# A one-core transformer block with a mixture of experts: the second half's routing and sort moved behind and between the experts' products, and the end without products that place x

## The chip, the cores and the metric

One NeuronCore of a Trainium2 chip runs the whole kernel. The metric is the time of one execution on the device in microseconds (us); the median of three runs is shown.

## What is computed

One block on 512 tokens of width 1024: a norm, an input projection, forgetting attention beside a gated recurrence, an output projection, and then a mixture of experts. The change touches the last part only:

```python
h2 = rmsnorm(x, ffn_norm[l]).reshape(b * s, d)
# hierarchical_moe: group_p = softmax(h2 @ w_group + b_group), the top 1 of 4 groups (weight g_w)
#   inner = h2 @ w_inner[group] + b_inner, softmax, the top 2 of 8 experts, renormed
for g in range(N_GROUPS):
    hg = silu(einsum('nd,edf->nef', t, w_gate[g])) * einsum('nd,edf->nef', t, w_up[g])
    y = y + einsum('nef,efd->nd', hg * combine[:, g, :, None], w_down[g])
x = x + y.reshape(b, s, d)
return rmsnorm(x, final_norm)
```

Each of the 32 experts has 3 MB of weights (gate, up, down: 1024 x 256 floats each), 100 MB in all, read once.

## The kernel before, in words

**Tokens and experts.** The tokens are four tiles t of 128, in two halves hf (t 0 and 1, t 2 and 3). For each half an expert has 32 places (CAP). The experts are worked off in eight quads (g, q) of four experts: g 0 is the first group; the other 24 experts are ranked by their load (`sort_parts`, L899), and the last group (LIGHT, the lightest) needs only one set of places for both halves. Should an expert get more tokens than places, a branch at the very end (L1297) works the rest off; the number `ovi` that decides it is made at L1285 to L1293.

**A quad.** `gather_parts` (L951) makes one-hot matrices s16 (f16) and s (fp32r) from the tokens' places and multiplies h2 with them, in four parts of two k-blocks each; h2 (scaled) is held as a high part h2h (fp32r, ACT) and a low part h2l (f16), so a part is eight products. The results go to the tile xg, evicted by DVE (parts 0 and 2) and ACT (1 and 3). `gate_up` multiplies xg with the gate and up weights, one k-block of 128 at a time (four experts a block; 8 blocks). `places` puts the one-hots and the weights c into the layout of the experts' rows (sT, cw), `hidden` is silu and product (ACT, DVE), `hidden_T` transposes it, `down` multiplies with w_down, `split_y` splits its result into two fp32r parts (ACT, DVE), `scatter` multiplies back to tokens and DVE adds to xs, which holds x.

**Routing.** `fill_router` (L624) makes a tile's router logits lg and h2; for t 3 the low part is an ACT copy h2s and a POOL subtraction (L656 to L659). `route(1)` (L679) ranks the second half's groups and experts (`ranks`, L670; go, o), makes the 0/1 mask msk, counts with products on PE (stri, onesb) the tokens before each token, which DVE turns into counts cnt and places pos1, and then computes the experts' weights c16. Its small tiles lie in the pool `work`.

**The order.** Where `pinned` is 1, PE's instructions stay in program order; with 2, those of DVE and ACT do as well. What comes between the router of t 3 and the loop over the quads is written in the string FIRST (L49, loop at L1135): "hk" is k-block k of half h of quad (0, 0), "gather" a part of half 1's gather, "rank" the counting products and the one-hots, "weights" the rest of route(1), the release of `work`, the pool `ring_b` in its place, and the loads of quad (0, 0)'s down weights, "sort" the next of the five parts of `sort_parts`. The loop over the quads (L1155) goes on with half 0's blocks 4 and up, places, hidden.

**Weights.** All weight loads stand on SP's queue in program order, as loads of 512 KB into slots of 1 MB: 12 in `slot`, 4 in `slot_m`, 2 in `slot_b`. slot_b lies in `ring_b`, over tiles of `work`. A load waits for its slot and for the one eight before it. The loads of a ranked expert need its number, which SP reads from `ids`, a result of the sort.

**The end** (L1240 to L1297). In the last quad four products `place_x` (one for each t, identity times x, the second 512 columns) put x into PSUM, between k-blocks 4 to 7; the last scatter adds to it there. `square_out` (L1076) sums squares on ACT, `rsqrt_parts` (L1094) makes the factors, `write_out` (L1082) scales and writes eight pieces of 256 KB. Four ACT copies then bring x back to xs for the branch, and the overflow number is made.

## Time and profile before

| | us |
|---|---|
| three runs: lowest, median, highest | 511.38, 511.52, 512.45 |
| the profiled execution | 510.38 |
| its span | 508.6 |
| PE (TensorE products) busy | 470.3 (92%) |
| DVE (VectorE) busy | 291.4 (57%) |
| ACT (ScalarE) busy | 193.5 (38%) |
| POOL (GpSimd) busy | 47.1 (9%) |

Clock granted to PE, mean over the span: 0.979. The DMA engines read 118.45 MB of HBM, at 237 GB/s over the span. Times in the rows below count from the span's start. An engine's idle time is put down to the one whose semaphore came last; idle time of an engine that others do not wait for costs nothing, and a share of busy time over the span says little about one stage, so stretches are read each by itself.

### The profile page before, as it was taken

Reading aid. Unit: us, or ns where it says so; the run is one execution under the profiler, and the core shown is the slowest. Engines: PE = TensorE matmul, PEld = TensorE weight load, DVE = VectorE, ACT = ScalarE, POOL = GpSimd, SP = SyncE. Lnnn points to the kernel's source line nnn. Section 1 sums busy time; section 2 is a strip of 40 time slices with the busy share of each in tenths; the row PEclk is TensorE's granted clock in tenths of the full one; section 3 lists DMA queues with packets and bytes.
Section 4 is the critical chain, followed back from the end, with each engine's and each line's share of the span. In section 5 each row is a group of like instructions: output and inputs, shape, how many; then the busy total and the mean of one; then the engine's idle time right before and its main releaser. Section 6 shows DMA issues by size and latency. Waiting matters only on the chain.

```text
span 508.6 us, 9411 instructions
## 1 busy us (share of the span) xinstructions
PE 470.3 (92%) x3525; PEld 287.0 (56%) x3525; DVE 291.4 (57%) x757; ACT 193.5 (38%) x406; POOL 47.1 (9%) x90
## 2 busy tenths in 40 slices
PE   7999999979999999999849999999999999998970
PEld 4997777758887877678414435434354333642330
DVE  4868654396996578967772525436263353353343
ACT  6454157736773357555402113111131111211045
POOL 4400000230121022300100000000000000000030
PEclk9999999999999999999879999999999999998996
DMA  8687332123244400327943999999999999999924
GB/s 315 108 205 197 81 86 78 47 75 93 83 145 187 167 0 1 100 69 275 381 170 117 386 378 378 417 409 410 404 386 409 406 413 371 388 411 382 333 104 168
DMA packets 58578, 121.20 MB, mean 238 GB/s; under 512 B 10753, under 2 KB 29217, under 8 KB 58530
## 3 DMA queue, kind: packets, MB, share of 16 engines
q1 hardware_dynamic: 58528, 120.56, 65.7%
q8 instruction: 29, 0.48, 0.4%
q14 instruction: 19, 0.16, 0.1%
q10 hardware_dynamic: 2, 0.00, 0.0%
HBM read 118.45 MB, written 2.10 MB: 237 GB/s over the span
## 4 chain that ended last, share of the span: by engine, by line
PE 81%; DVE 10%; ACT 6%; issue 1%; DMA 1%; POOL 0%; DVEq 0%; ACTq 0%; POOLq 0%
PE ps_mm L69 46%; PE ps_lg L69 17%; PE ps_tr L69 10%; PE ps_pv L69 4%; PE ps_tr L79 3%; DVE hold L393 1%; DVE hg L88 1%; ACT hold L94 1%; ACT slot L94 1%; DMA xs<-in_x_dram 1%; DVE srt L82 1%; ACT hg L94 1%; DVE s L82 1%; DVE slot L82 0%; DVE msk L88 0%
## 5 line engine op out<-in xcount | busy, mean ns | idle before, releaser
L69 PE MATMUL ps_mm<-slot 128*128 128x512 f32 (+1 forms) x576 | 120.3, 366 | 2.9 <-DVE kS L82 2.8
L69 PE MATMUL ps_mm<-slot,xg 128*32 128x512 f32 x688 | 106.6, 613 | 7.2 <-DVE xg L82 6.6
L69 PEld LDWEIGHTS ps_mm<-slot 128*128 128x128 f32 x576 | 96.2, 192 | 22.2 <-issue 5.1
L69 PEld LDWEIGHTS ps_mm<-slot,xg 128*32 128x32 f32 x688 | 26.6, 112 | 45.5 <-issue 35.6
L82 DVE TENSOR_TENSOR xs<-xs,ps_lg 128x512 f32<-128x512 f32 x56 | 34.8, 682 | 12.4 <-PE ps_lg L69 12.2
L82 DVE TENSOR_TENSOR slot<-slot 128x1024 fp32r<-128x1024 f32 (+1 forms) x27 | 32.9, 1221 | 13.4 <-ACT slot L94 13.4
L94 ACT ACTIVATE hg<-ps_mm 128x256 f32<-128x256 f32 x14 | 5.4, 383 | 89.1 <-PE ps_mm L69 83.8
L88 DVE SCALAR_TENSOR_TENSOR hg<-hg,ps_mm 128x256 f32<-128x256 f32 x14 | 5.9, 421 | 56.2 <-ACT hg L94 56.2
L94 ACT ACTIVATE y<-ps_tr 128x512 fp32r<-128x512 f32 x26 | 15.5, 597 | 49.8 <-PE ps_tr L69 38.2
L69 PE MATMUL ps_lg<-y,sT 128*128 128x512 f32 x118 | 33.4, 421 | 1.1 <-ACT y L94 0.9
L69 PE MATMUL ps_lg<-s,hold 128*128 128x256 f32 x128 | 33.3, 367 | 0.5 <-ACT s L94 0.4
L69 PE MATMUL ps_lg<-s,h2l 128*128 128x256 f16 x128 | 32.2, 285 | 0.9 <-DVE s L82 0.9
L94 ACT ACTIVATE slot<-slot 128x1024 fp32r<-128x1024 f32 (+1 forms) x28 | 29.3, 1055 | 6.8 <-DMA slot<-in_w_in_dram 5.0
L69 PEld LDWEIGHTS ps_lg<-y,sT 128*128 128x128 f32 x118 | 19.9, 188 | 20.6 <-issue 10.9
L82 DVE TENSOR_TENSOR y<-ps_tr,y 128x512 fp32r<-128x512 f32 x26 | 17.9, 687 | 21.9 <-ACT y L94 21.9
L558 POOL TENSOR_TENSOR ql<-qT,qh 64x128 fp32r<-64x128 f32 x32 | 19.9, 622 | 110.5 <-ACT qh L94 96.3
L69 PE MATMUL ps_mm<-slot_m,xg 128*32 128x512 f32 x128 | 28.9, 593 | 0.0
L1080 POOL TENSOR_TENSOR slot<-xs,gfin 128x512 f32<-128x512 f32 x4 | 5.0, 1282 | 241.2 <-ACT slot L94 241.2
L69 PEld LDWEIGHTS ps_lg<-s,hold 128*128 128x128 f32 x128 | 26.0, 203 | 2.3 <-ACT s L94 2.3
L69 PE MATMUL ps_mm<-slot,hold 128*128 128x512 f32 x96 | 26.2, 409 | 0.0
L69 PE MATMUL ps_mm<-slot,oT 128*128 128x512 f32 x96 | 24.6, 402 | 0.5 <-DVE oT L82 0.5
L94 ACT ACTIVATE xg<-ps_lg,g8s 128x256 f32<-128x256 f32 x28 | 11.7, 470 | 33.0 <-PE ps_lg L69 32.9
(269 smaller groups left out, 747.2 us busy)
## 6 DMA issues: line engine op xcount, KB each, us to landing
slot<-in_w_gate_dram SPq DMA_DIRECT2D x50, 512.0 KB, 10.1
slot<-in_w_up_dram SPq DMA_DIRECT2D x50, 512.0 KB, 10.2
slot_m<-in_w_down_dram SPq DMA_DIRECT2D x24, 512.0 KB, 10.1
slot<-in_w_down_dram SPq DMA_DIRECT2D x24, 512.0 KB, 10.7
slot<-in_w_in_dram SPq DMA_DIRECT2D x16, 512.0 KB, 3.9
slot<-in_w_out_dram SPq DMA_DIRECT2D x8, 512.0 KB, 3.9
slot_m<-in_w_gate_dram SPq DMA_DIRECT2D x8, 512.0 KB, 11.4
slot_m<-in_w_up_dram SPq DMA_DIRECT2D x8, 512.0 KB, 10.7
```

Source lines behind the costliest of these rows:

```text
L69: pin(nc.tensor.matmul(out=out_, lhsT=lhsT, rhs=rhs, start=start, stop=stop))
L79: pin(nc.tensor.transpose(out=out_, in_=in_, identity=ident[0:n, 0:n]))
L82: return pin(nc.vector.tensor_tensor(out=out_, in0=a, in1=b, op=op), 2)
L88: pin(nc.vector.scalar_tensor_tensor(out=out_, in0=a, scalar=s, in1=b, op0=op0, op1=op1), 2)
L94: pin(nc.scalar.activation(out=out_, in_=in_, func=func, **kw), 2)
L393: nc.vector.tensor_tensor_scan(out=ti_[:, c, :], data0=tr_[:, c, :], data1=xc[:, c, :], initial=0.0, op0=ALU.mult, op1=ALU.add)
L558: nc.gpsimd.tensor_tensor(out=ql[own, hh], in0=src, in1=qh[own, hh].bitcast(F32), op=ALU.subtract)
L1080: nc.gpsimd.tensor_tensor(out=yo[t][:, sl], in0=src, in1=gfin[:, sl], op=ALU.mult)
```

## The change

1. FIRST is rewritten: six k-blocks of half 0 ahead of "rank", which now also finishes the router of t 3 (r3), releases `work`, opens `ring_b` and starts quad (0, 0)'s down loads; "sort" is the first two parts at once, and "weights" is what remains of route(1), behind the gathers and 13.
2. The low part of h2 of t 3 is one DVE instruction behind the one-hots, as for the other t, instead of ACT's h2s and POOL's subtraction.
3. route(1)'s small tiles move from `work` to the pool `moe` (under tags that are free then), so `ring_b` no longer lies over them; mg and the group's Exp come right behind msk.
4. The last three parts of the sort (the places of groups 1 to 3, posp) become `sort_places(g + 1)`, called in the pass with q 1 ahead of each group; the sort's middle part (light, more, over) and the overflow number stand in pass 1.
5. A gather's products for the second t of a half take the high part first; half 1's first gather is evicted by ACT alone.
6. Quad (0, 0)'s gate and up weights come with two k-blocks to a load (32 loads of 256 KB) instead of four (16 of 512 KB).
7. At the end place_x and the four copies go; the last scatter is added to xs by DVE; the first half of the second down product stands right behind the first down; PSUM tags follow.

```diff
-FIRST = "00 01 02 03 rank 04 05 weights sort gather sort 06 10 11 gather sort 12 gather sort 07 13 gather sort"
+FIRST = "00 01 02 03 04 05 rank 06 07 gather gather 10 11 sort gather 12 13 weights gather"
...
         if t == 3:
-            v = kd(w4("h2s"))
-            act(v, x_kp, AF.Copy, scale=invs[:, 0:1])
-            nc.gpsimd.tensor_tensor(out=lo, in0=v, in1=hi.bitcast(F32), op=ALU.subtract)
-        else:
-            stt(lo, x_kp, invs[:, 0:1], hi.bitcast(F32), ALU.mult, ALU.subtract)
+            yield
+        stt(lo, x_kp, invs[:, 0:1], hi.bitcast(F32), ALU.mult, ALU.subtract)
...
+        def two_bytes(shape, dt, name):
+            if hf:
+                return moe[0].tile(shape, dt, name=name, tag="hgT", bufs=2)
+            return work.tile(shape, dt, name=name, tag="msk" if name == "msk" else "si", bufs=1)
+        small_ = moe[0].tile([P, 136], F32, name="rt", tag="hg", bufs=1) if hf else work.tile([P, 136], F32, name="rt", bufs=1)
...
+    def sort_places(g):
+        r0 = first_rank(g)
+        t_ = ring_b[0].tile([P, 5, EG, NS], F16, name="sp", tag="y0", bufs=2)
+        sh = [P, NT, EG, NS]
+        p1 = pos1.rearrange("p t g e -> p t (g e)")[:, :, EG:]
+        tt(t_[:, 0], bc(rank1[0], [P, EG, NS], 1), bc(iota1[:, r0:r0 + EG], [P, EG, NS], 2), ALU.is_equal)
+        tt(t_[:, 1:], bc(p1, sh, 2), bc(t_[:, 0], sh, 1), ALU.mult)
+        with nc.allow_low_precision(reason="one number of a sum isn't zero"):
+            pin(nc.vector.reduce_sum(out=posp[0][:, :, r0:r0 + EG], in_=t_[:, 1:], axis=AX.X), 2)
...
-                terms = [(h, t, i) for h in hfs for t in range(2) for i in range(2)]
+                terms = [(h, t, i) for h in hfs for t in range(2) for i in ((0, 1), (1, 0))[t]]
...
-            if kk % 2:
+            if kk % 2 or by_act:
...
-    gus[0] = load_gate_up(experts(0, 0), 4)
+    gus[0] = load_gate_up(experts(0, 0), 2)
...
         if o == "rank":
             next(r1)
             s01 = next(g01)
-        elif o == "weights":
-            run(r1)
+            run(r3)
             work.release()
             ring_b.append(pool("ring_b"))
             dns[0] = load_down(experts(0, 0))
             sx[0, 1] = s01, next(g01)
+        elif o == "weights":
+            run(r1)
+        elif o == "sort":
             srt = sort_parts()
-        elif o == "sort":
+            next(srt)
             next(srt)
...
+            if i == 1:
+                run(srt)
+                ovf = small.tile([P, 1], F32, name="ovf", bufs=1)
...
+            if q == 1:
+                sort_places(g + 1)
             gu_k(0, range(4, KT))
...
-        if k >= 4:
-            place_x(k - 4, "pv" if k == 7 else "lg")
...
+    py1 = psum("tr")
+    down_mm(py1, hgT, dns[i], 1, [0])
+    pa, pb = ([psum("lg"), psum(tag)] for tag in ("lg", "mm"))
...
+    down_mm(py1, hgT, dns[i], 1, [1])
+    y1 = split_y(py1)
...
+    for t in range(2):
+        scatter_add(pc[t], t, 1)
+        square_out(t, 1, xs[:, t, h1])
+    for t in range(2):
+        scatter_add(pd[t], 2 + t, 1)
...
-    for t in range(NT):
-        act(xs[:, t, h1], pz[t], AF.Copy)
```

How the order of the engines moves, at the two places that the prediction speaks of and at the end. PE from the router of t 3 on: `ps_tr<-wr,h2T` is the router's product, `ps_mm<-slot,xg` with four products to a k-block the gate/up products, stri and onesb the counting products, `ps_lg<-s,...` a gather with the low part (h2l) and the high one (hold). Before:

```order
L69 MATMUL ps_tr<-wr,h2T 128x36 x8
L69 MATMUL ps_mm<-slot,xg_2523 32x512 x16
L69 LDWEIGHTS stri
L69 MATMUL ps_tr<-msk,stri 128x32
...
L69 MATMUL ps_tr<-msk,onesb 128x24
L69 MATMUL ps_mm<-slot,xg_2523 32x512 x8
L69 LDWEIGHTS h2l
L69 MATMUL ps_lg<-s_2664,h2l 128x256
L69 MATMUL ps_lg<-s_2663,hold_2441 128x256
```

and with the change:

```order
L69 MATMUL ps_tr<-wr,h2T 128x36 x8
L69 MATMUL ps_mm<-slot,xg_2530 32x512 x24
L69 LDWEIGHTS stri
L69 MATMUL ps_tr<-msk,stri 128x32
...
L69 MATMUL ps_tr<-msk,onesb 128x24
L69 MATMUL ps_mm<-slot,xg_2530 32x512 x8
L69 LDWEIGHTS h2l
L69 MATMUL ps_lg<-s_2671,h2l 128x256
L69 MATMUL ps_lg<-s_2670,hold_2432 128x256 x2
```

Six k-blocks stand ahead of the counting products instead of four, two behind them as before, and the gather takes its two high parts in a row.

DVE behind the counting products (cnt and pos read them; s is the one-hot, srt, rank, idf, ids the sort, xg the first gather's eviction). Before, the last of the sort and what follows it:

```order
L82 TENSOR_TENSOR c_1058<-go,cp 128x192
L82 TENSOR_TENSOR s_2664<-iota_500,pos_1057 128x256 x2
L88 SCALAR_TENSOR_TENSOR srt_2720<-cnt_1061,iota_500 128x24
...
L85 TENSOR_SCALAR ids<-idf 1x24
L931 TENSOR_REDUCE over<-pos_1057 128x1
...
L939 TENSOR_REDUCE posp<-srt_2774 128x4x8
L939 TENSOR_REDUCE posp<-srt_2791 128x4x8
...
L939 TENSOR_REDUCE posp<-srt_2813 128x4x8
L85 TENSOR_SCALAR ovf<-ovf 128x1
L82 TENSOR_TENSOR xg_2719<-ps_lg,g8s 128x512 x2
```

and with the change:

```order
L88 SCALAR_TENSOR_TENSOR msk<-rt 128x32 x2
L709 TENSOR_REDUCE rt<-lg 128x2
L82 TENSOR_TENSOR rt<-lg,rt 128x8
L82 TENSOR_TENSOR cnt_1061<-ps_tr,cnt_1060 128x24
L88 SCALAR_TENSOR_TENSOR pos_1057<-ps_tr,msk 128x64
L82 TENSOR_TENSOR s_2671<-iota_500,pos_1057 128x256 x2
L88 SCALAR_TENSOR_TENSOR h2l<-xs,invs,hold_2432 128x1024
L88 SCALAR_TENSOR_TENSOR srt_2732<-cnt_1061,iota_500 128x24
...
L85 TENSOR_SCALAR ids<-idf 1x24
L85 TENSOR_SCALAR rt<-rt 128x16 x2
```

The one-hots s come ahead of the weights (c), the low part h2l behind them, the sort up to ids next, then the weights (the small rt); posp and xg are gone from this stretch.

PE at the end, from the last gate/up products on (hgT stands in the down products, y in the scatter). Before:

```order
L69 MATMUL ps_mm<-slot,xg_4536 32x512 x2
L69 MATMUL ps_pv<-xs,ident 128x512
L69 MATMUL ps_tr<-ident,hg 32x128 x8
L69 MATMUL ps_mm<-slot,hgT 32x512 x8
L69 MATMUL ps_mm<-y_5032,sT_4959 128x512
L69 MATMUL ps_mm<-y_5033,sT_4959 128x512
```

and with the change:

```order
L69 MATMUL ps_mm<-slot,xg_4546 32x512 x2
L69 MATMUL ps_tr<-ident,hg 32x128 x8
L69 MATMUL ps_mm<-slot,hgT 32x512 x8
L69 MATMUL ps_tr<-slot,hgT 32x512 x4
L69 MATMUL ps_lg<-y_5034,sT_4969 128x512
L69 MATMUL ps_lg<-y_5035,sT_4969 128x512
```

The last place_x (ps_pv from xs) is gone, and four of the second down's products stand ahead of the first scatter.

## Rows read from the trace of the kernel before

**Rows 1.** The page: the busy line of TensorE (busy us, share of the span, instructions), the GB/s of the 40 slices, and from its DMA issues the last down's sixteen loads (count, KB each, median us from issue to landing).
```profile
PE 470.3 (92%) x3525; PEld 287.0 (56%) x3525; DVE 291.4 (57%) x757; ACT 193.5 (38%) x406; POOL 47.1 (9%) x90
...
GB/s 315 108 205 197 81 86 78 47 75 93 83 145 187 167 0 1 100 69 275 381 170 117 386 378 378 417 409 410 404 386 409 406 413 371 388 411 382 333 104 168
...
slot<-in_w_down_dram SPq DMA_DIRECT2D x16, 256.0 KB, 5.6
```

**Rows 2.** Busy time by stretches of 4 us around the second half's routing: the stretch, its length, busy us and instructions (x) of PE, PEld, DVE, ACT and POOL, the granted clock of PE as a share, the DMA engines' busy share and GB/s.
```profile
248.00:252.00 4.00, 1.77 (x19) 1.29 (x19) 3.45 (x11) 0.28 (x2) 2.34 (x1) 0.92 1.02 413
252.00:256.00 4.00, 3.57 (x20) 1.35 (x12) 3.62 (x18) 0.75 (x2) 0.00 (x0) 0.65 0.64 236
...
260.00:264.00 4.00, 0.07 (x4) 0.07 (x8) 3.88 (x8) 0.00 (x0) 0.00 (x0) 0.70 0.32 119
264.00:268.00 4.00, 4.00 (x19) 0.93 (x20) 0.00 (x0) 0.00 (x0) 0.00 (x0) 0.50 0.00 0
```

**Rows 3.** PE's timeline there: start us, us, engine, line, operation, out<-in, tile, count, and in brackets the idle time before it and who ended it. `ps_mm<-slot,xg` are gate/up products, `ps_tr<-msk,stri` is the first of rank's, `ps_lg<-ident,s` begins places, `ps_pv<-ident,hg` is hidden_T.
```profile
244.63 3.64 PE L69 MATMUL ps_mm<-slot,xg 128*32 128x512 f32 x32
250.51 0.19 PE L69 MATMUL ps_tr<-msk,stri 128*128 128x32 bf16 x1 [2.23 <-DVE msk L88]
...
250.76 3.63 PE L69 MATMUL ps_mm<-slot,xg 128*32 128x512 f32 x16
...
263.93 3.64 PE L69 MATMUL ps_mm<-slot,xg 128*32 128x512 f32 x16 [6.59 <-DVE xg L82]
...
269.69 1.07 PE L69 MATMUL ps_mm<-slot,xg 128*32 128x512 f32 x8 [0.62 <-ACT xg L94]
...
274.67 0.29 PE L69 MATMUL ps_lg<-ident,s 128*32 128x128 f16 x8
...
277.43 0.61 PE L69 MATMUL ps_pv<-ident,hg 128*32 128x128 f32 x16
```

**Rows 4.** The chain of waits, in order of time, at one gather part that ran without a wait (start us, us, what).
```profile
270.75 1.07 PE ps_lg L69 x8
```

**Rows 5.** The timelines of DVE, ACT and POOL, columns as in rows 3: the first half's msk, the low part of another t, and what the second half's routing has on these engines.
```profile
208.38 0.58 DVE L88 SCALAR_TENSOR_TENSOR msk<-o,go 128x32 bf16<-128x32 f32 x2
...
235.34 2.31 DVE L88 SCALAR_TENSOR_TENSOR h2l<-xs,invs,hold 128x1024 f16<-128x1024 f32 x1 [2.41 <-ACT hold L94]
...
243.03 0.84 ACT L94 ACTIVATE xg<-ps_lg,g8s 128x256 f32<-128x256 f32 x2 [1.28 <-PE ps_lg L69]
...
248.06 2.34 POOL L659 TENSOR_TENSOR h2l<-h2s,hold 128x1024 f16<-128x1024 f32 x1 [36.72 <-ACT h2s L94]
...
248.19 2.37 DVE L88 SCALAR_TENSOR_TENSOR msk<-o,go 128x32 bf16<-128x32 f32 x2
...
254.21 0.76 DVE L82 TENSOR_TENSOR s<-iota,pos 128x256 f16<-128x256 f16 x2
...
258.80 0.17 DVE L85 TENSOR_SCALAR ids<-idf 1x24 int32<-1x24 f32 x1
...
259.96 1.81 DVE L939 TENSOR_REDUCE posp<-srt 128x32 f16<-128x768 f16 x2
...
263.20 0.68 DVE L82 TENSOR_TENSOR xg<-ps_lg,g8s 128x512 f32<-128x512 f32 x1
```

**Rows 6.** The timeline of SP's DMA queue (the time is that of the issues): half 0's last weights, the first and last of the loads into slot_b, the next one, and the last quad's down weights.
```profile
213.37 0.43 SPq L104 DMA_DIRECT2D slot<-in_w_up_dram  x1
...
253.96 0.33 SPq L104 DMA_DIRECT2D slot_b<-in_w_gate_dram  x1
...
255.28 0.77 SPq L104 DMA_DIRECT2D slot_b<-in_w_up_dram  x1
273.69 0.33 SPq L104 DMA_DIRECT2D slot<-in_w_gate_dram  x1
...
466.98 14.38 SPq L104 DMA_DIRECT2D slot<-in_w_down_dram  x16
```

**Rows 7.** Busy time by stretches of 100 us, columns as in rows 2: most of the quads.
```profile
284.00:384.00 100.00, 98.77 (x964) 44.52 (x952) 46.11 (x104) 20.80 (x47) 0.00 (x0) 1.00 1.02 399
384.00:484.00 100.00, 95.64 (x897) 38.27 (x896) 39.98 (x97) 15.59 (x36) 0.00 (x0) 0.98 1.01 389
```

**Rows 8.** PE's timeline, columns as in rows 3: two hidden_T in the quads that waited.
```profile
342.80 0.64 PE L69 MATMUL ps_pv<-ident,hg 128*32 128x128 f32 x16 [0.85 <-DVE hg L88]
...
461.46 0.64 PE L69 MATMUL ps_pv<-ident,hg 128*32 128x128 f32 x16 [1.62 <-DVE hg L88]
```

**Rows 9.** Busy time of one microsecond behind the second of them, columns as in rows 2.
```profile
463.00:464.00 1.00, 1.00 (x9) 0.22 (x4) 0.00 (x0) 0.00 (x0) 0.00 (x0) 0.51 1.13 352
```

**Rows 10.** The chain of waits at the end, in order of time. `ps_lg x2` at 481.35 is a place_x; `ps_mm x16` are the two downs.
```profile
481.35 1.06 PE ps_lg L69 x2
...
486.07 2.05 PE ps_mm L69 x16
...
491.41 1.98 PE ps_mm L69 x16
...
502.84 1.95 ACT xs L94 x4
...
505.05 0.15 DVE ovi L1293
```

**Rows 11.** Busy time of one microsecond near the end, columns as in rows 2.
```profile
506.00:507.00 1.00, 0.00 (x0) 0.00 (x0) 0.00 (x0) 0.00 (x0) 0.00 (x0) 0.50 0.01 2
```

More of the change, by code (lines that the diff above doesn't have):

```diff
@@ L645, in fill_router @@
         yield
-        invs = work.tile([P, 1], F32, name="invs", bufs=2)
+        invs = (moe[0] if t == 3 else work).tile([P, 1], F32, name="invs", bufs=1 if t == 3 else 2)
         ts(invs, inv, H2S, ALU.mult)
@@ L694, in route @@
         ts(go, go, 0.0, ALU.is_equal)
-        ranks(o1, il, EG)
+        ranks(o1, il, EG, two_bytes)
         yield
-        msk = work.tile(s4d, BF16, name="msk", bufs=1)
+        msk = two_bytes(s4d, BF16, "msk")
         for t in range(2):
             stt(msk[:, t], bc(o1[:, t], [P, NG, EG], 1), 2.0, bc(go[:, t], [P, NG, EG], 2), ALU.is_lt, ALU.mult)
+        pin(nc.vector.reduce_max(out=mg, in_=lgg, axis=AX.X), 2)
+        tt(eg, lgg, mg.broadcast_to([P, 2, NG]), ALU.subtract)
+        act(eg, eg, AF.Exp)
         yield
@@ L730, in route @@
         tt(m1, m1, gw, ALU.mult)
-        nc.vector.reciprocal(out=m1, in_=m1)
+        pin(nc.vector.reciprocal(out=m1, in_=m1), 2)
         tt(m2, m2, m1, ALU.mult)
@@ L735, in route @@
         tt(o1, o1, o2, ALU.add)
-        cp = work.tile([P, 2, 3, EG], F16, name="cp", tag="si", bufs=1)
+        cp = two_bytes([P, 2, 3, EG], F16, "cp")
         ts(cp[:, :, 0], o1, CS, ALU.mult)
@@ L933, in sort_parts @@
         posp.append(moe[0].tile([P, NT, NS], F16, name="posp", bufs=1))
-        for r0 in range(0, NS, EG):
-            sh = [P, NT, EG, NS]
-            v = y_tile(0, sh, F16)
-            tt(v, bc(p1, sh, 2), bc(oh[:, r0:r0 + EG], sh, 1), ALU.mult)
-            with nc.allow_low_precision(reason="one number of a sum isn't zero"):
-                pin(nc.vector.reduce_sum(out=posp[0][:, :, r0:r0 + EG], in_=v, axis=AX.X), 2)
-            yield
+        yield
+    def sort_places(g):
[7 more added lines that the diff above has]
+            pin(nc.vector.reduce_sum(out=posp[0][:, :, r0:r0 + EG], in_=t_[:, 1:], axis=AX.X), 2)
     def place_of(g, t):
@@ L1124, in block_kernel @@
     next(r3)
+    pinned[0] = 2
     r1 = route(1)
+    next(r3)
     for _ in range(3):
         next(r1)
-    run(r3)
     pg1 = pst("gu")
@@ L1192, in block_kernel @@
                     held.pop()()
+            if i == 1:
+                run(srt)
+                ovf = small.tile([P, 1], F32, name="ovf", bufs=1)
+                ones_ = small.tile([P, 1], F32, name="ones_", bufs=1)
+                nc.vector.memset(ones_, 1.0)
+                tt(ovf, over[:, 0:1], over[:, 1:2], ALU.max)
+                ts(ovf, ovf, float(CAP), ALU.is_gt)
+                pt = pst("tr")
+                mm(pt[0:1, 0:1], ovf, ones_, True, True)
+                ovi = small.tile([1, 1], I32, name="ovi", bufs=1)
+                nc.vector.tensor_copy(out=ovi, in_=pt[0:1, 0:1])
+            if q == 1:
+                sort_places(g + 1)
             gu_k(0, range(4, KT))
@@ L1224, in block_kernel @@
     h0, h1 = slice(0, 512), slice(512, D)
-    pz = []
-    def place_x(t, tag):
-        pz.append(psum(tag))
-        mm(pz[t], ident, xs[:, t, h1], True, False)
     pg = pst("gu")
@@ L1262, in block_kernel @@
         scatter_add(pb[t], 2 + t, 0)
+    down_mm(py1, hgT, dns[i], 1, [1])
+    y1 = split_y(py1)
     for t in range(2, 4):
         square_out(t, 0, xs[:, t, h0])
[L1265 to L1279 removed]
+    pc, pd = ([psum("lg"), psum(tag)] for tag in ("mm", "tr"))
+    scatter_to(pc, y1, sT[0])
+    scatter_to(pd, y1, sT[1])
+    n0, n1 = (rsqrt_parts(hf) for hf in range(2))
+    for t in range(2):
[3 more added lines that the diff above has]
+        scatter_add(pd[t], 2 + t, 1)
+    i0 = next(n0)
+    run(n0)
+    for t in range(2, 4):
+        square_out(t, 1, xs[:, t, h1])
+    write_out(0, 1, i0, xs[:, 0, h1])
+    i1 = next(n1)
+    run(n1)
     for t in range(NT):
[L1281 removed]
+        if t:
+            write_out(t, 1, (i0, i1)[t // 2], xs[:, t, h1])
+        write_out(t, 0, (i0, i1)[t // 2], None)
     pinned[0] = 0
[L1285 to L1293 removed]
     ps.release()
```

69 lines of the change are left out of this document (21 added, 48 removed).

## The prediction

> **What bounds the kernel now.** I read the page first, then the stretches of 4 us around the start of the second half's routing, then each engine's timeline there, then the DMA queue and the chain of waits at the end. TensorE is busy for 92% of the span [rows 1], so time can come only from stretches where it stands still, runs at the low clock, or does work that is taken out. There are two such stretches. The first lies at 248 to 272 us: PE is busy for 1.77 us of 248:252 and 0.07 us of 260:264, its clock is 0.65 in 252:256 and 0.50 in 264:268, and the DMA engines, which carry the weights, move nothing in 264:268 [rows 2]. The second is the end, after the last gate/up product.
>
> The first stretch is a chain through VectorE. From the start of half 0's first gate/up products (244.63) to the first hidden_T (277.43) pass **32.80 us** [rows 3]. The products between them, at full clock, are fifteen k-blocks (eight of half 0's first eight, four of half 1, three more) at 3.64/4 = 0.91 us, four gather parts at 1.07 [rows 4], rank's products 0.25 (250.51 to 250.76) and places 0.3 (274.67): 13.65 + 4.28 + 0.25 + 0.3 = **18.5 us**. The missing 14.3 us are read off the same rows: 2.23 us of waiting for msk, 6.59 us for DVE's xg, 0.62 us for ACT's xg, and twice 1.8 us because 250.76 and 263.93 ran sixteen instructions in 3.63 us where 244.63 ran thirty-two in 3.64. These are 13.0 us; the rest is small hand-overs.
>
> Why the waits are there: the two msk instructions take 2.37 us instead of 0.58 [rows 5] while POOL subtracts h2l for 2.34 us beside them. And DVE comes to gather's xg (263.20) only after weights, sort and three posp, which stand ahead of it in its order. At the end, the chain holds four place_x products of 1.06 us (481.35 is one pair), and four ACT copies (1.95 us), ovf's product and its cast stand behind the last scaling [rows 10].
>
> **The change, part by part, on PE.** Six k-blocks now come ahead of rank: 244.63 + 6 × 0.91 = 250.1. msk no longer shares its time with POOL: even from the old start of 248.19 it ends at 248.8, so the 2.23 us wait is covered with 1.3 us to spare. Rank's products end at 250.35 and 06, 07 at 252.15.
>
> DVE then does cnt and pos (0.3), s16 (0.76, the 254.21 row) until 251.5, and now h2l. It has no row for half 3, but the same instruction took 2.31 us at 235.34, so h2l is ready at 253.85. The first gather does three products (0.4) and waits from about 252.55 to 253.85: a **new wait of 1.3 to 1.45 us** that replaces POOL's work. Gather ends at 254.5, the next at 255.6, 10 and 11 at 257.4, the third at 258.5, 12 and 13 at 260.3, the fourth at 261.4, places at 261.8, three k-blocks at 264.5. With 0.3 us of hand-overs hidden_T is at 264.8 against 277.43: **12.6 us earlier**. Bounds: 10.8 if the clock falls after the new wait, 14.0 if h2l costs no wait.
>
> Off PE: the first two sort parts (from the end of s16 at 254.97 to 258.97 before, 4.0 us) follow h2l and end near 257.6, where ids was written at 258.97 [rows 5], so SP's reads of it are not late. The route's weights follow, some 4.5 us of small instructions ending in c near 262.2. Places needs c at 261.5 to 261.8, and its product with c comes last, so up to 0.4 us may be lost; hidden's DVE work would then be at 264.0, where PE comes to it at 264.5. ACT now evicts all of half 1's parts, 0.84 us each (the 243.03 row) against at least 1.07 of PE per part: hidden. Swapping the gather terms moves nothing in the sum of products.
>
> Three posp pieces move into later passes. Each pass gets about 1.8 us of DVE (a posp pair took 1.81 us for two); the first also gets the rest of the sort and ovf, 2.7 us in all. In 284:384 DVE is busy 46 of 100 us [rows 7], and by the order PE's next product that needs DVE in that pass, ovf's, comes after four or more k-blocks. I cost this at nothing; if that cover is gone, it costs up to 1.8 us in three passes and 2.7 in one.
>
> **The weight stream** must keep up. Before, slot_b's loads began at 253.96, since the ring lies over tiles that cp (on DVE) still used; the loads then stopped from 255.28 until 273.69, when the slots of half 0 came free [rows 6]. Now the ring's last earlier user is a rank product at about 250.4. Half 0's slots come free in two pieces, after 11 (257.4) and after 13 (260.3). The stream runs 13.4 to 16.3 us earlier, and PE, at the last down products, 12.6 + 3.2 = 15.8 us earlier. From 284 on the DMA engines are full (share 1.02 and 1.01, [rows 7]), so nothing can be caught up. The sixteen loads of the last down are issued from 466.98 to 481.36 [rows 6]; those for its first half, the first eight, are issued well ahead of use at 486.07 [rows 10]. I cost this at nothing, with up to 2 us in the range.
>
> Half 0's own weights now come in 32 loads of 256 KB instead of 16 of 512 KB. The last was issued at 213.37 and used from 244.63: 31 us of cover. Sixteen more issues of 0.43 us [rows 6] are 7 us. This is hidden. The Trainium skill speaks against it: "DMA: Bandwidth & Descriptors", section "Bandwidth", says to batch transfers to at least 1 MiB, and its section "Anatomy of one DMA" puts a fixed cost of about 2 us on each. By that page my estimate would be 16 × 2 = 32 us more if the loads went one after another, which would use up the cover. The trace shows loads of 512 KB that reach 399 GB/s [rows 7], with the next ones issued before the last have landed; I keep it as a rival.
>
> **The end.** Three place_x ahead of hidden go: 3 × 1.06 = 3.2 us (the fourth lies beside ACT and DVE). The first half of the second down goes into the wait for the split y0 that follows the first down (486.07 + 2.05): half of the 1.98 us at 491.41, so that the scatter of the second half starts 4.2 us earlier. Against this, four DVE additions (0.68 each, the shape of the 263.20 row) stand ahead of the squares that read PSUM before; by my walk the last output is scaled near 498.9 against 502.84, 3.9 earlier. Behind the last scaling the copies, the product and the cast are gone (502.84 to 505.20, 2.4 us), and what remains is the output's transfer: bytes moved until just past 506 (2 GB/s in 506:507, [rows 11]), some 2.4 us before the end. With the last byte at 502.0 the end is 504.4; if the end hangs on the last engine as it did on the cast (3.4 us from 505.2), it is 502.4. So 4.2 to 6.2 us; I take **5.0**, nearer the byte end.
>
> **Sum.** 12.6 + 5.0 = 17.6. The profiled execution took 510.38 us (span 508.6), 1.14 below the median 511.52. 510.38 − 17.6 = 492.8, and 1.14 more gives **493.9 us**. Its own range, from the bounds above (12.6 + 6.2 and 10.8 + 4.2 or so, less half a microsecond of places), is 491.5 to 497.
>
> **Rivals.**
> (a) *The clock falls after the new wait.* The wait of 1.62 us at 461.46 [rows 8] was followed by a clock of 0.51 in 463:464 [rows 9], and the wait of 2.23 us by one of 0.65 [rows 2]; the wait of 0.85 at 342.80 [rows 8] was not. 1.3 to 1.45 us lies between. Then 1.8 us are lost once more, as at 263.93: 495.7. Chance 0.17.
> (b) *The weights arrive late.* The stream gains only some 10 us because a slot or SP's read of ids holds it, and the last down waits 3.7 us: 497.6. For it: no spare bandwidth from 284 on. Against it: PE waited for few weights before, and both new release points are ahead of the old one. Chance 0.13.
> (c) *DVE is late* for c and hg in the first pass and in the passes with posp: about 3 us in all, 497. Chance 0.07.
> (d) *Slower: the stream's rate decides.* Seven quads of 12.58 MB, less four loads of 0.52 already issued, are 86 MB. If they begin at 257.4, and the end comes 20.5 us after the last lands (before, the last was issued by 481.36 and landed near 486.3, where the median of its sixteen is 5.6 us [rows 1]; that is 22.3 before the end, less 1.8 of the end's gain), then at 371 GB/s, the lowest of the quads' slices but the last in [rows 1], they take 231.8 us and the span is 509.7: the turning point. At 365 the span would be 513.5 and the median 516.4. Slices of 378 to 417 stand against it. Chance 0.03. The same page of the Trainium skill, in "Specifications", limits a core to about 358 GB/s of HBM (its share of a pair's, says "Bandwidth"); by it my estimate would be 240 us for 86 MB and 518 for the span. The trace does not agree: 399 and 389 GB/s in [rows 7].
> (e) *Half 0's smaller loads are late* by 4 us for 06 and 07: 498. Chance 0.03; 24 us of cover remain by the rows.
> (f) *The change does not do what it says:* slot_b and the following loads stay held until c. Then PE gains only about 6 us in the middle: 501. Chance 0.02.
>
> **How the numbers follow.** The forecast has 0.55. The range 489.5 to 499.5 holds (a), (b), (c), (e) and the forecast with the ends at their best together (14.0 + 6.2); it leaves out (d), (f) and some of the tails. About 0.2%, or 1 us, is what a measurement of this kernel can tell from no change. Every case but (d), and (d) only near its turning point, is faster by more: faster 0.95, same 0.02, slower 0.03.
>
> **What the changed profile should show.** msk near 0.6 us in all; no wait of PE above 2 us in 244 to 266, and one of about 1.4 at the first gather; hidden_T near 264.8; SP issuing again near 257; no ps_lg<-xs,ident at the end; the last PE product some 17 us earlier. A low clock at 255 to 259, PE waits on slot loads in 270 to 475, or hidden_T past 268 would show a step wrong.

## The result and the profile after

The changed kernel took **492.53 us** (median of four runs, 491.60 to 492.85) against 511.45 for the kernel before beside it (511.12 to 512.45): a ratio of 0.9624, 95% interval 0.9605 to 0.9643, or 19 us less. The forecast was 493.9. Run once more with the last set of experiments it took 492.44. The profiled execution took 492.85 us, its span is 491.1 (508.6 before).

The stretches that answer to [rows 2], in the changed kernel: but for one wait in 252:256 PE is busy throughout, at the full clock of 2.4 GHz (1.00; 0.50 is 1.2 GHz, called the low clock below), and the DMA engines never stop.

```profile
248.00:252.00 4.00, 4.00 (x41) 1.00 (x33) 1.76 (x6) 0.96 (x3) 0.00 (x0) 1.00 1.01 398
252.00:256.00 4.00, 3.08 (x30) 1.96 (x30) 3.83 (x7) 1.62 (x4) 0.00 (x0) 1.00 1.05 418
...
260.00:264.00 4.00, 4.00 (x64) 1.94 (x66) 2.60 (x12) 1.39 (x4) 0.00 (x0) 1.00 1.02 392
264.00:268.00 4.00, 4.00 (x76) 1.60 (x69) 1.86 (x6) 1.25 (x3) 0.00 (x0) 1.00 1.00 366
```

PE's timeline that answers to [rows 3] (start us, us, engine, line, operation, out<-in, tile, count, idle time before and who ended it). From the first gate/up products to the first hidden_T it is now 263.66 − 244.68 = 18.98 us, where it was 32.80. Of the waits only one of 0.92 us at the first gather is left.

```profile
244.68 5.36 PE L69 MATMUL ps_mm<-slot,xg 128*32 128x512 f32 x48
249.97 0.19 PE L69 MATMUL ps_tr<-msk,stri 128*128 128x32 bf16 x1
...
250.18 1.92 PE L69 MATMUL ps_mm<-slot,xg 128*32 128x512 f32 x16
...
253.47 0.39 PE L69 MATMUL ps_lg<-s,h2l 128*128 128x256 f16 x2 [0.92 <-DVE h2l L88]
...
263.66 0.61 PE L69 MATMUL ps_pv<-ident,hg 128*32 128x128 f32 x16
```

DVE there, answering to [rows 5]: msk takes 0.29 us, h2l 2.10, ids is written at 257.41, and c at 261.70.

```profile
247.52 0.29 DVE L88 SCALAR_TENSOR_TENSOR msk<-rt 128x32 bf16<-128x32 f32 x2
...
250.64 0.76 DVE L82 TENSOR_TENSOR s<-iota,pos 128x256 f16<-128x256 f16 x2
251.32 2.10 DVE L88 SCALAR_TENSOR_TENSOR h2l<-xs,invs,hold 128x1024 f16<-128x1024 f32 x1
...
257.24 0.17 DVE L85 TENSOR_SCALAR ids<-idf 1x24 int32<-1x24 f32 x1
...
261.34 0.36 DVE L82 TENSOR_TENSOR c<-rt,cp 128x192 f16<-128x192 f32 x1
```

SP's queue, answering to [rows 6]: slot_b is loaded from 250.33 and the next slots from 257.06, against 253.96 and 273.69.

```profile
250.33 0.33 SPq L104 DMA_DIRECT2D slot_b<-in_w_gate_dram  x1
...
257.06 0.33 SPq L104 DMA_DIRECT2D slot<-in_w_gate_dram  x1
...
448.81 0.33 SPq L104 DMA_DIRECT2D slot<-in_w_up_dram  x1
451.21 14.37 SPq L104 DMA_DIRECT2D slot<-in_w_down_dram  x16
```

Where the 17.5 us of the span lie, by marks that both traces have (ACT's hg is the start of hidden, the last mark ahead of the end):

| stretch | before | after | difference |
|---|---|---|---|
| first gate/up products to first hidden_T | 32.80 | 18.98 | −13.8 |
| to hidden_T of the last quad but one (461.46; 447.17) | 184.0 | 183.5 | −0.5 |
| to ACT's hg of the last quad (483.47; 463.91) | 22.0 | 16.7 | −5.3 |
| to the end of the span | 25.1 | 27.2 | +2.1 |

The rows of hg, before (from the chain of waits) and with the change:

```profile
483.47 0.39 ACT hg L94
```

```profile
463.91 0.38 ACT L94 ACTIVATE hg<-ps_mm 128x256 f32<-128x256 f32 x1 [3.73 <-PE ps_mm L69]
```

The third line is more than the three place_x (3.2 us). PE's rows behind the hidden_T of the last quad but one tell the rest: in both kernels it waits 1.62 and 0.54 us, but the thirty-two down products behind it took 5.34 us before and 3.64 after. The first is the row of before, the other two are of after; [rows 8] has the wait of before. The kernel before:

```profile
462.64 5.34 PE L69 MATMUL ps_tr<-slot_m,hgT 128*32 128x512 f32 x32 [0.54 <-DVE hgT L91]
```

The changed kernel:

```profile
447.17 0.64 PE L69 MATMUL ps_pv<-ident,hg 128*32 128x128 f32 x16 [1.62 <-DVE hg L88]
448.35 3.64 PE L69 MATMUL ps_tr<-slot_m,hgT 128*32 128x512 f32 x32 [0.54 <-DVE hgT L91]
```

The fourth line is a loss. The last hidden_T now waits 1.57 us and not 0.42, since no place_x stands there, and in this execution PE ran at 0.50 behind it: the first down, 1.92 us before, took 3.38.

```profile
465.41 0.65 PE L69 MATMUL ps_tr<-ident,hg 128*32 128x128 f32 x16 [1.57 <-DVE hg L88]
466.60 3.38 PE L69 MATMUL ps_mm<-slot,hgT 128*32 128x512 f32 x16 [0.54 <-DVE hgT L91]
469.73 1.34 PE L69 MATMUL ps_tr<-slot,hgT 128*32 128x512 f32 x8
```

In another execution of the same kernel (x_again) the same wait was followed by the full clock:

```profile
465.72 0.65 PE L69 MATMUL ps_tr<-ident,hg 128*32 128x128 f32 x16 [1.57 <-DVE hg L88]
466.91 1.92 PE L69 MATMUL ps_mm<-slot,hgT 128*32 128x512 f32 x16 [0.54 <-DVE hgT L91]
```

And the output is no sooner out. Its first transfer is issued at 481.09, 17.2 us behind hg (499.61 before, 16.1 behind); bytes move until 488.3, and the span ends 2.8 us later. SP's queue, before and with the change:

```profile
499.61 4.49 SPq L1089 DMA_DIRECT2D out_dram<-slot  x8
```

```profile
481.09 5.52 SPq L1102 DMA_DIRECT2D out_dram<-slot  x8
```

The last microseconds in which the changed kernel moves bytes:

```profile
487.00:488.00 1.00, 0.00 (x0) 0.00 (x0) 0.00 (x0) 0.00 (x0) 0.00 (x0) 0.50 1.02 387
488.00:489.00 1.00, 0.00 (x0) 0.00 (x0) 0.00 (x0) 0.00 (x0) 0.00 (x0) 0.50 0.27 100
```

### The profile page after: what moved, and what is told of

Read it like the earlier page. It is cut to its first block, busy times and chain, and to the rows that moved or that the text cites. A ratio compares the mean times of both kernels' runs of the same rounds, so it can differ in the third digit from the quotient of the medians.

```text
span 491.1 us, 9425 instructions
## 1 busy us (share of the span) xinstructions
PE 459.8 (94%) x3517; PEld 284.5 (58%) x3517; DVE 294.0 (60%) x763; ACT 191.4 (39%) x405; POOL 44.7 (9%) x89
## 4 chain that ended last, share of the span: by engine, by line
PE 84%; DVE 9%; ACT 4%; issue 1%; DMA 1%; POOL 0%; DVEq 0%; ACTq 0%; POOLq 0%
PE ps_mm L69 48%; PE ps_lg L69 18%; PE ps_tr L69 11%; PE ps_pv L69 4%; PE ps_tr L79 3%; DVE hold L393 1%; DVE hg L88 1%; DVE h2l L88 1%; ACT hold L94 1%; DMA xs<-in_x_dram 1%; DVE s L82 1%; ACT hg L94 1%; DVE xs L82 1%; DVE slot L88 0%; DVE slot L82 0%
## 5 line engine op out<-in xcount | busy, mean ns | idle before, releaser
L69 PE MATMUL ps_mm<-slot,xg 128*32 128x512 f32 x688 | 102.1, 594 | 0.0
L82 DVE TENSOR_TENSOR xs<-xs,ps_lg 128x512 f32<-128x512 f32 x61 | 38.1, 683 | 13.4 <-PE ps_lg L69 13.2
L69 PE MATMUL ps_lg<-y,sT 128*128 128x512 f32 x122 | 35.0, 422 | 1.1 <-ACT y L94 0.9
L94 ACT ACTIVATE y<-ps_tr 128x512 fp32r<-128x512 f32 x27 | 16.1, 598 | 48.6 <-PE ps_tr L69 36.8
L69 PE MATMUL ps_lg<-s,hold 128*128 128x256 f32 x128 | 30.5, 323 | 0.6 <-ACT s L94 0.6
L69 PE MATMUL ps_lg<-s,h2l 128*128 128x256 f16 x128 | 26.9, 278 | 1.5 <-DVE h2l L88 0.9
L69 PE MATMUL ps_tr<-slot,hgT 128*32 128x512 f32 x208 | 25.8, 601 | 0.0
L94 ACT ACTIVATE pe<-ps_lg,nb 128x128 f32<-128x128 f32 (+3 forms) x32 | 16.8, 526 | 18.2 <-DVE nb L85 13.0
```

What stands on the lines that cost most here:

```text
L69: pin(nc.tensor.matmul(out=out_, lhsT=lhsT, rhs=rhs, start=start, stop=stop))
L82: return pin(nc.vector.tensor_tensor(out=out_, in0=a, in1=b, op=op), 2)
L94: pin(nc.scalar.activation(out=out_, in_=in_, func=func, **kw), 2)
```

## The experiments

Each is the changed kernel or the one before with one thing changed, run at least five times beside the kernel before on the same chip. Times are medians; a ratio is to the kernel before in the same set (511.07, 510.9 and 511.31). Each was profiled in one execution. The first gate/up products start anywhere from 244.14 to 245.35 in these profiles, so they are compared below by stretches and not by times from the span's start.

**x_end: the end alone.** The kernel before, with the changed kernel's code from the last quad on, but with the overflow number still behind the last write.

```diff
-        if k >= 4:
-            place_x(k - 4, "pv" if k == 7 else "lg")
...
+    py1 = psum("tr")
+    down_mm(py1, hgT, dns[i], 1, [0])
...
-    for t in range(NT):
-        act(xs[:, t, h1], pz[t], AF.Copy)
```

> The kernel before with the change's end alone (no place_x, no copies, the first half of the second down ahead of the first scatter); everything ahead of the last quad stays, and the overflow number stays behind the last write. By the prediction's term for the end: 5.0 us less than before, 506.4. By the two traces (place_x gives 3.2 us, but from ACT's hg on the changed kernel takes 27.2 us where before took 25.1): 1.1 less, 510.3. If the low clock behind hidden's longer wait is what costs there, and it does not come in this kernel: about 2.9 less, 508.5.

Measured: 509.29 us, ratio 0.9956 (0.9940 to 0.9971), 1.5 to 3.1 us faster, where the three readings gave 5.0, 1.1 and 2.9: the prediction's 5.0 is excluded for all but the overflow number. From the hidden_T of the last quad but one to hg it takes 18.7 us (22.0 before), which is what three place_x give. Its trace has the low clock in both last quads: behind the 1.62 us wait of the last but one, as before has, and in the last, whose two rows take 1.92 and 1.04 at the full clock.

```profile
482.48 0.64 PE L69 MATMUL ps_tr<-ident,hg 128*32 128x128 f32 x16 [1.45 <-DVE hg L88]
483.67 2.82 PE L69 MATMUL ps_mm<-slot,hgT 128*32 128x512 f32 x16 [0.55 <-DVE hgT L91]
486.25 1.91 PE L69 MATMUL ps_tr<-slot,hgT 128*32 128x512 f32 x8
```

**x_mid: everything but the end.**

```diff
-    py1 = psum("tr")
-    down_mm(py1, hgT, dns[i], 1, [0])
...
+        if k >= 4:
+            place_x(k - 4, "pv" if k == 7 else "lg")
...
+    for t in range(NT):
+        act(xs[:, t, h1], pz[t], AF.Copy)
```

> The changed kernel with the end of before (place_x and the four copies back). By the prediction's term for the middle, 12.6 us: 498.9. By the two traces, hidden_T 13.8 us earlier and another 0.5 in the passes: 497.2; and if the low clock that before had at 463 to 467 (1.7 us) stays away, as in the changed kernel's trace: 495.5. In its trace the wait ahead of the last hidden_T should be 0.4 us, not 1.6, and the clock there full.

Measured: 495.12 us, ratio 0.9684 (0.9665 to 0.9703): 15.2 to 17.1 us from the middle, and 2.6 more with the changed end. Its last hidden_T waits 0.42 us, and the down behind it takes 1.92. It has the overflow number in pass 1 and the copies behind the last write, and from hg (467.92) to the end it takes 25.5 us, no less than the 25.1 before: the number's product and cast cost nothing where they stood.

```profile
469.33 0.65 PE L69 MATMUL ps_tr<-ident,hg 128*32 128x128 f32 x16 [0.42 <-DVE hg L88]
470.52 1.92 PE L69 MATMUL ps_mm<-slot,hgT 128*32 128x512 f32 x16 [0.55 <-DVE hgT L91]
```

**x_fill: one unread product in the last wait.**

```diff
             sT, cw = places(g, q, (0, 1), sx[g, 0][0])
+    mm(psum("pv"), ident, xs[:, 3, h1], True, True)
     gfin = ring_b[0].tile([P, D], F32, name="gfin", tag="xg1", bufs=1)
```

> The changed kernel with one product of 128x512 put into an unused PSUM bank between the last gate/up product and hidden_T of the last quad, where PE waits 1.57 us for hg; its result is not read. If the low clock behind that wait comes from the wait's length: the wait falls to about 0.5 us, the second of 3.38 us becomes 1.92, and the time falls by 1.8 us to 490.7. If the clock falls for another reason (the later waits for hgT and y): no change, 492.5. If the product delays hidden_T: later, 493.0.

Measured: 491.34 us (490.92 to 492.39), ratio 0.9618 (0.9599 to 0.9636). The trace does what the first theory says, the time moves by 1.1 us instead of 1.8, and the interval overlaps with that of the changed kernel (0.9639, 0.9620 to 0.9658, in its second set), so the gain is not settled. Nor does the trace settle that the product kept the clock up, since x_again has the full clock there without it; from hg to the end x_again then takes 25.9 us and x_fill 25.5.

```profile
463.46 1.13 PE L69 MATMUL ps_pv<-xs,ident 128*128 128x512 f32 x2
465.01 0.65 PE L69 MATMUL ps_tr<-ident,hg 128*32 128x128 f32 x16 [0.42 <-DVE hg L88]
466.21 1.92 PE L69 MATMUL ps_mm<-slot,hgT 128*32 128x512 f32 x16 [0.55 <-DVE hgT L91]
```

**x_fill2: one in the quad before as well.**

```diff
-            hgT = hidden_T(hidden(pgs[0], cw))
+            hg = hidden(pgs[0], cw)
+            mm(pst("gz"), ident, xs[:, 0, 512:], True, True)
+            hgT = hidden_T(hg)
```

> The changed kernel with a product whose result is not read in both last waits for hidden: one of 128x512 ahead of the last hidden_T (as in the run before) and one ahead of the hidden_T of the quad before it, where PE waits 1.62 us. If the low clock follows the longer wait at either place, now in one execution and now in another: both stay at full clock in the profile and the median falls to 490.9 with a smaller spread, against 492.5 of the changed kernel and 491.3 with one product. If the clock falls whatever the wait: 492, with a spread of 1.5 us as before.

Measured: 491.51 us (490.69 to 492.20), ratio 0.9617 (0.9601 to 0.9634). The wait fell from 1.62 to 0.57 us and both places show the full clock in the profiled execution, but neither median nor spread is better than with one product: a miss. That the spread of 1.5 us comes from elsewhere is not shown, since the other four executions have no profile; the longest of them has the lowest mean clock, 0.988 against 0.990 and 0.991.

```profile
447.06 0.65 PE L69 MATMUL ps_pv<-ident,hg 128*32 128x128 f32 x16 [0.57 <-DVE hg L88]
```

**x_pool: h2l back on ACT and POOL.**

```diff
         if t == 3:
-            yield
-        stt(lo, x_kp, invs[:, 0:1], hi.bitcast(F32), ALU.mult, ALU.subtract)
+            v = kd(w4("h2s"))
+            act(v, x_kp, AF.Copy, scale=invs[:, 0:1])
+            nc.gpsimd.tensor_tensor(out=lo, in0=v, in1=hi.bitcast(F32), op=ALU.subtract)
+        else:
+            stt(lo, x_kp, invs[:, 0:1], hi.bitcast(F32), ALU.mult, ALU.subtract)
```

> The changed kernel with the low part of h2 of the last token tile back on ACT (a copy) and POOL (the subtraction), as before; everything else as in the change. If DVE's instruction is what the first gather waits for: h2l is ready near 252, the wait of 0.92 us goes and DVE's sort starts 2.1 us sooner, 491.6. If POOL's subtraction slows what DVE does beside it, as it did msk (2.37 us instead of 0.58): the one-hots are 1 to 1.5 us late instead, and the time is 492.5 to 493.5.

Measured: 492.95 us, ratio 0.9643 (0.9620 to 0.9666): no difference from the change. The rows of DVE and POOL show why: the two one-hots now take 1.85 us beside POOL's subtraction, where they took 0.76, and PE's first gather is as late as with h2l on DVE (hidden_T at 263.55). DVE:

```profile
250.79 1.85 DVE L82 TENSOR_TENSOR s<-iota,pos 128x256 f16<-128x256 f16 x2
```

POOL:

```profile
249.64 2.38 POOL L659 TENSOR_TENSOR h2l<-h2s,hold 128x1024 f16<-128x1024 f32 x1 [38.09 <-ACT h2s L94]
```

The Trainium skill has this: "SBUF — State Buffer", section "Who interferes with whom", says that a DVE instruction with two inputs in SBUF contends with a GpSimd instruction that reads SBUF. The rows agree, here and for msk in [rows 5].

**x_rank4: rank behind four k-blocks.**

```diff
-FIRST = "00 01 02 03 04 05 rank 06 07 gather gather 10 11 sort gather 12 13 weights gather"
+FIRST = "00 01 02 03 rank 04 05 06 07 gather gather 10 11 sort gather 12 13 weights gather"
```

> The changed kernel with rank back behind four k-blocks of half 0 (00 to 03, as before) and 04 to 07 behind it; nothing else is moved. By the changed trace msk is ready at 247.8, ahead of the end of four k-blocks (248.3), since POOL no longer runs beside it: no wait at rank, h2l ready 1.8 us sooner, the first gather's wait of 0.92 us gone, 491.6. If the two extra k-blocks are what covers rank's wait, as the prediction's step says: a wait of 1 to 2 us ahead of rank, 493 to 494.5.

Measured: 493.92 us (492.15 to 494.74), ratio 0.9653 (0.9631 to 0.9675): slower than the change by 1.4, if at all, and for neither reason given. There is no wait at rank: msk is done at 248.02 and its product starts at 248.47, right behind the four blocks. The first gather does not wait either, and hidden_T comes at 262.80. That is 17.90 us behind the first products, 1.1 less than in the change. But in the last quad PE waits for the up weights, and the down products of the quad before ran at the low clock (5.18 us).

```profile
248.47 0.19 PE L69 MATMUL ps_tr<-msk,stri 128*128 128x32 bf16 x1
...
262.80 0.61 PE L69 MATMUL ps_pv<-ident,hg 128*32 128x128 f32 x16
...
447.47 5.18 PE L69 MATMUL ps_tr<-slot_m,hgT 128*32 128x512 f32 x32 [0.54 <-DVE hgT L91]
...
462.43 0.59 PE L69 MATMUL ps_mm<-slot,xg 128*32 128x512 f32 x1 [0.52 <-DMA slot<-in_w_up_dram]
```

**x_kc4: half 0's weights in 16 loads.**

```diff
-    gus[0] = load_gate_up(experts(0, 0), 2)
+    gus[0] = load_gate_up(experts(0, 0), 4)
```

> The changed kernel with half 0's weights back in 16 loads of 512 KB (four k-blocks each), so that their slots come free behind 13 (260.2) and not behind 11 (257.1). If the weights have no slack left, as the prediction's sum for the stream says (13.4 to 16.3 us sooner against 15.8 for PE): all later loads land 3.1 us later, the last gate/up load at 462 against PE's use at 460.2, and the time is 494.4. If the slots bind nothing: 492.5. If smaller loads cost the stream time by themselves, as the rule on 1 MiB says: earlier than 492.5.

Measured: 494.96 us, ratio 0.9696 (0.9671 to 0.9720), 2.5 us slower than the change. SP goes on at 260.44 and not at 257.06, the last up weights are issued at 451.49 instead of 448.81, and PE waits for them 1.15 us; from the hidden_T of the last quad but one to the last hidden_T it takes 20.4 us, where x_again, at the same clock, takes 18.2. SP's queue:

```profile
260.44 0.33 SPq L104 DMA_DIRECT2D slot<-in_w_gate_dram  x1
...
451.49 0.33 SPq L104 DMA_DIRECT2D slot<-in_w_up_dram  x1
```

PE in the last quad, and the load that it waits for:

```profile
462.94 0.59 PE L69 MATMUL ps_mm<-slot,xg 128*32 128x512 f32 x1 [1.15 <-DMA slot<-in_w_up_dram]
```

**x_earlyfill: h2l in DVE's idle time ahead of rank.** With x_fill's product.

```diff
     for _ in range(3):
         next(r1)
+    next(r3)
     pg1 = pst("gu")
```

> The changed kernel with DVE's low part of h2 right behind msk and the group's difference, where DVE stands idle for 2.2 us until rank's products (no order on PE is changed), and with the one unread product ahead of the last hidden_T. The first gather's wait of 0.92 us should go, and hidden_T come 0.9 us sooner. If PE's chain alone sets the time: 490.4. If the weights are the second bound right behind it, as the 16 larger loads and rank behind four blocks showed: PE waits for the last quad's up weights instead, and the time is that of the one product alone, 491.3, or later.

Measured: 492.10 us (490.02 to 493.36), ratio 0.9610 (0.9586 to 0.9634). PE's middle is as short as x_rank4's, 17.90 us (hidden_T at 262.04), with no wait at the gather, but in the profiled execution (493.36) PE waits 1.57 us for the last up weights and gives it back. The other four took 490.02 to 492.22; whether they waited there too, no profile shows.

```profile
262.04 0.61 PE L69 MATMUL ps_pv<-ident,hg 128*32 128x128 f32 x16
...
461.23 0.59 PE L69 MATMUL ps_mm<-slot,xg 128*32 128x512 f32 x1 [1.57 <-DMA slot<-in_w_up_dram]
```

**x_sortfront: the whole sort in front.**

```diff
             run(r1)
+            run(srt)
+            for g_ in range(1, 4):
+                sort_places(g_)
...
-            if q == 1:
-                sort_places(g + 1)
```

> The changed kernel with all of the sort in front again: the rest of it and the three posp pieces right behind the weights in FIRST, none in the passes. They are some 6 us of DVE, of which about 1.5 us come ahead of each of the first two hidden by the order. By the prediction, which costs the moved pieces at nothing where they went: hidden_T 1.5 us later at the first and up to 1.5 more at the second, 494 to 495.5. If DVE has room here too: 492.5.

Measured: 497.48 us (494.63 to 497.76), ratio 0.9711 (0.9684 to 0.9737). Both first hidden_T wait for DVE, and PE loses 2.8 us by the second. Of the rest against the change's profile, 1.7 us are the low clock in the last quad but one (5.33 us) and 0.5 lie ahead of the first gate/up products; in the last quad both have the low clock (3.10 and 3.38).

```profile
265.86 0.65 PE L69 MATMUL ps_pv<-ident,hg 128*32 128x128 f32 x16 [1.51 <-DVE hg L88]
...
270.38 0.65 PE L69 MATMUL ps_pv<-ident,hg 128*32 128x128 f32 x16 [0.54 <-DVE hg L88]
```

**x_bydve: parts 0 and 2 evicted by DVE.**

```diff
-    g01 = gather_parts(0, 1, True)
+    g01 = gather_parts(0, 1)
```

> The changed kernel with parts 0 and 2 of half 1's first gather evicted by DVE again. DVE then stands before the sort until the first part is done and does 1.4 us more: c some 2 us later. By the prediction's walk DVE is 0.4 us ahead of PE at the first hidden, so hidden_T comes 1.5 to 2 us later: 494.2. If DVE has room there: 492.5.

Measured: 494.56 us, ratio 0.9676 (0.9658 to 0.9693), 2.1 us slower than the change. hidden_T waits 1.07 us for DVE at 265.45, 20.2 us behind the first products (19.0 in the change). That is 1.2 us of the 2.1; the profiled execution also has the low clock in the last quad but one.

```profile
265.45 0.65 PE L69 MATMUL ps_pv<-ident,hg 128*32 128x128 f32 x16 [1.07 <-DVE hg L88]
...
450.13 5.34 PE L69 MATMUL ps_tr<-slot_m,hgT 128*32 128x512 f32 x32 [0.54 <-DVE hgT L91]
```

**x_again and x_halfout.** The change itself, and x_fill with half of the output not written (it leaves out the first 512 columns):

```diff
-        nc.sync.dma_start(out=out_v[:, t, sl], in_=yo[t][:, sl])
+        if n:
+            nc.sync.dma_start(out=out_v[:, t, sl], in_=yo[t][:, sl])
```

> The changed kernel itself, once more, on the same chip and beside the others of this set: 492.5, between 491.6 and 493. It is what the next two are compared with.

> The changed kernel with the one unread product, and with the first 512 columns of the output not written (scaled, but no transfer): four output transfers of 256 KB instead of eight. If the end is set by the output's transfer, 2.1 MB at some 380 GB/s from the first write on, and not by the last scaling, as the kept 2.7 us behind the last byte suggest: the last transfer starts with the last scaling (482.5) and the span ends near 487.5, 1.6 us earlier than with all eight: 489.7. If the end is set by the last scaling alone: 491.3.

Measured: x_again 492.44 us, ratio 0.9639 (0.9620 to 0.9658); x_halfout 490.21 us (489.76 to 490.39), ratio 0.9590 (0.9573 to 0.9608), 1.1 us less than x_fill. Both theories are half right: without half of the transfer the end is earlier, but by less than 1.6. By the traces it is 1.4 us from hg to the end (25.5 and 24.1), although x_halfout scales later: one small DVE instruction takes 0.96 us beside POOL's last multiplication (0.15 in x_fill, where POOL is done by then). With all eight transfers x_fill's last bytes move 4 us behind its last scaling (482.5), and the span ends 6.6 us behind it; with four they move 2 us behind it (483.7), and it ends 4.4 us behind it. The stretches of one microsecond show it, x_fill first (columns as in [rows 2], GB/s last):

```profile
485.00:486.00 1.00, 0.00 (x0) 0.00 (x0) 0.00 (x0) 0.00 (x0) 0.00 (x0) 0.50 1.00 381
486.00:487.00 1.00, 0.00 (x0) 0.00 (x0) 0.00 (x0) 0.00 (x0) 0.00 (x0) 0.50 0.39 143
```

x_halfout:

```profile
485.00:486.00 1.00, 0.00 (x0) 0.00 (x0) 0.00 (x0) 0.00 (x0) 0.00 (x0) 0.50 0.50 180
486.00:487.00 1.00, 0.00 (x0) 0.00 (x0) 0.00 (x0) 0.00 (x0) 0.00 (x0) 0.50 0.03 10
```

## Why the prediction was right, and where it was not

**The sum was right, its two terms were not.** 12.6 + 5.0 was forecast; x_mid, the middle alone, gave 16.0 (15.2 to 17.1), and the end gave 2.6 on top of it, or 1.8 by itself in x_end. The two errors, +3.4 and −2.4, nearly cancel: that the total came so close is luck. The range is not worked out right either: 12.6 + 6.2 gives 492.7, and its lower end of 491.5 needs some 14.0 + 6.2.

**The middle's mechanism held, its size was a little low.** hidden_T came 13.8 us earlier, not 12.6. The wait at the first gather was 0.92 us, not 1.3 to 1.45, since h2l took 2.10 us and not 2.31, the hand-overs that I added did not show, and the products took 18.1 us and not 18.5. c was there at 261.70 and hg at 263.44, just ahead of PE (263.66): the slack of 0.4 us was 0.2, and x_bydve shows what passes it. The two profiled executions differ by 15.2 us (spans 508.6 and 493.4): 14.4 up to the hidden_T of the last quad but one, and 1.7 us of low clock behind it that x_mid's and the change's profiles do not have and that of before has, less 0.7 of late weights in x_mid's last quad and some small terms. The low clock was not in my sum at all, and how much of it the medians hold no profile shows.

**One step of it failed.** I put the end of rank's wait down to msk without POOL and to two more k-blocks of cover; by my numbers msk (248.8) would still have come 0.5 us behind four blocks (248.3). x_rank4 takes the two blocks away and there is no wait: without POOL beside it, msk is done (248.02) ahead of four blocks. And h2l on DVE by itself is worth nothing in the new order (x_pool): POOL's subtraction slows the one-hots by as much as DVE's instruction makes the gather wait. What the step gets right is only that msk and POOL's subtraction must not overlap.

**The moved sort** was costed at nothing where it went and is: from the first hidden_T to that of the last quad but one PE waits for hg five times for 4.1 us in all, before and after. In front it costs 2.8 us (x_sortfront). Evicting by ACT is worth 2.1 us by the medians, of which the trace shows 1.2 (x_bydve); I had called it hidden, which is so, and given no price for its absence.

**The weight stream** (rival b) is not the bound in the changed kernel, but it stands right behind PE. In three profiles PE waits for the last quad's up weights: 0.52 us in x_rank4 and 1.57 in x_earlyfill, whose PE came 1.1 us sooner, and 1.15 in x_kc4, whose loads came later. In x_mid a weight load of PE at 460.65 waits 0.59 us for a DMA, so some 0.7 of the 2.6 us between x_mid and the change need not be the end's. PE's gain is not the whole of it: in x_earlyfill the last up load is issued at 451.00, 2.2 us later than in the change (448.81), though its stream went on 0.7 us sooner (256.34 against 257.06). In x_fill2, with the same loads in the same order, it comes at 446.56: the slack is not the same in every execution, and why is open. My sum had next to no slack by 16.3 against 15.8, and called it nothing "with up to 2 us in the range"; the runs bear out that range. The smaller loads help, as their slots come free sooner. The Trainium skill's rule of 1 MiB ("DMA: Bandwidth & Descriptors", section "Bandwidth") points the other way; x_kc4 measured 2.5 us in favour of 256 KB here, where half 0's loads have some 30 us of cover. The 2 us for each load that the prediction took from the same page are given there for loads that GpSimd issues, and these are SP's; the wait for 06 and 07 that they would have made did not come.

**The end's term was mis-sized.** Of 5.0, the 3.2 for three place_x came (3.3 in x_end). The other 1.8 were to come behind hg, and there the change's profile loses 2.1. Part of that is the clock. The fourth place_x stood in PE's wait for hidden. With a product there (before, x_mid, x_fill, x_fill2, x_earlyfill, x_halfout) the wait is 0.4 us and the down behind it took 1.92 us in all six profiles; without it the wait is about 1.5 us, and the clock behind it was low in three profiles of eight (the change, x_end, x_sortfront). This fits a product that keeps the clock up but does not show it: three falls among fourteen profiles would all lie on that side by chance about once in six or seven times.

The rest would have failed at the full clock too. From hg to the end the other five profiles without a product take 25.6 to 26.1 us, x_fill 25.5, and before 25.1. The walk itself held: in x_fill (hg at 463.60) the last scaling ends 18.9 us behind hg and before 19.4, so 0.5 us sooner, where I had 0.7. What failed is the step from there to the end. I let the last byte move as much sooner as the last scaling, and counted the copies, the product and the cast as time at the end. But before, the copies already ran beside the transfer, the last output byte moved just before 506, and the span ended 2.6 us later; in x_fill the eight transfers take 5.5 us to issue instead of 4.5, and the last byte moves some 22.8 us behind hg, against 22.5 before. x_halfout shows that the transfer takes part of the time there: 1.1 us in the median for half of it, 1.4 in the trace.

**Rival (a)**, the low clock behind the gather's wait, did not come: 0.92 us were followed by 1.00 in 252:256. But the same idea decides elsewhere, as (a)'s own row at 461.46 might have told me: at that wait of 1.62 us the down products took 5.2 to 5.34 us in six of the thirteen profiles that have it, before among them, and 3.64 in seven. I took it as the same in both kernels, and it is not the same in two executions of one chain. What sets it in one execution is open. So is how much of the forecast's success it makes, as before's profile has the low clock there and the change's has not. Rival (c) did not come, but by a slack of 0.2 us. Rival (e) is excluded by the row at 250.18: PE takes 06 and 07 in 1.92 us, without a wait. Rivals (d) and (f) are excluded: slot_b and the next loads came when the order said, and the stream ran at 399 and 386 GB/s in the same two windows of 100 us, shifted to 268:368 and 368:468.

**Left open:** whether x_fill or x_earlyfill is faster than the change (medians 491.34 and 492.10 against 492.44 and 492.53, with intervals that overlap), whether a product in the last wait keeps the clock up, and why x_rank4 is not faster, beyond what its profiled execution shows.
